# A gated hybrid block on one core: the first tile's convolution projection by seven products and at the end, the second tile's tokens scaled by way of DRAM, and pairs of units at the tile change

## The chip, the core and the metric

The kernel runs on one core of a Trainium2 chip. The metric is the device time of one execution in microseconds; the time of a kernel is the median of its runs. Engines are named as in the profile: PE is the matrix engine (TensorE), PEld its weight loads, DVE is VectorE, ACT is ScalarE, POOL is GpSimd and SP is SyncE, which here only issues DMAs. ACT and POOL issue DMAs too.

## The reference

One layer of a decoder block over 2048 positions and 1024 channels, in float32. Cut to what matters:

```python
h = rms_norm(x, norm_g)                                   # the scaled tokens
u = einsum('bsd,dc->bsc', h, w_in)                        # one input projection, split into:
v_c, b_c, c_c, z_c, q, k, v, z_a, gate_logits = split(u)
y_c = b_c * causal_depthwise_conv(c_c * v_c, conv_w)      # branch A: short gated convolution
y_c = y_c * silu(z_c)
y_a = y_c @ w_conv_out                                    # the convolution projection
q, k = rms_norm(q, q_norm_g), rms_norm(k, k_norm_g)       # branch B: attention over a window of 128
o = sliding_window_attention(q, k, v, sinks) * silu(z_a)
y_b = o @ w_attn_out                                      # the attention projection
g_a, g_b = split(sigmoid(gate_logits + gate_b))
return x + (g_a * y_a + g_b * y_b) @ w_out
```

## The kernel before, in words

**Precision.** Each operand is split into a high part (a cast on ACT) and a low part (a subtraction on DVE), and each block product is three matmuls: high by high, high by low, low by high. `op_split` and `form` make the operands ("op" tiles, 28 buffers), `two` inside `pieces_of` makes the weights' parts (8 buffers of 128x1024).

**Seven products.** A unit is a 1024 x 256 block of a weight matrix against the 1024 tokens of a tile. With both sides in halves it needs eight half products; the kernel forms sums of halves on DVE and does it in seven (Winograd's form of Strassen's scheme). One *product* is one of the seven: four blocks of 128 by three matmuls, 12 matmuls of 128x512. `sunit` runs one unit's seven products in turn; `spair` runs two units in turn about, in the order 1, 2, 5, 6, 3, 7, 4. The operand sides of the seven, numbered 1 to 7, come from four raw quarters and from `first_sum`, `second_sum`, `third` and `last_sum`.

**Tiles and stages.** The 2048 positions are two tiles of 1024 (T), each with halves of 512 (H). For each tile the units run in this order: k and v (tile 0 has a by-token form of its own), q (4), the convolution's c, v and b (12), the branch gates `ga` and `gb` (8), the convolution's gate `z` (4), the attention's gate `za` (4), the attention projection `yb` (4), the convolution projection `ya` (4). The attention's 32 blocks of a tile lie between the products from q to z. After both tiles comes the output projection `o` (8 units). `y_a` and `y_b`, multiplied by their gates, are added up in DRAM (`mt`): `yb` is stored by SP, `ya` is added by a DMA that accumulates, issued by POOL. The gated convolution result `y_c` goes through DRAM (`ocd`).

**The convolution projection of tile 0** is the one that is not done by seven: `ya_unit`, `branch` and `mm_t` (L1467) run eight half sums per unit from 16 plain operands (`opa`), 96 matmuls per unit. In tile 1, `ya` goes by `y_units`, `spair` and `sunit`; its sums of quarters are made ahead in `csum` and kept in DRAM (`csd`), and `conv_op` loads them by POOL's queue.

**Order.** The order on every engine is the program's order, written out by hand: `put(n, f)` places work at tick n, and `run` advances one tick for each product, so a tick is one product of PE with what is placed beside it. At each tick `run` also takes one *piece* of weight preparation (`piece`) from a list that runs ahead of the units: the raw weights (1 MB for a unit, two buffers) are loaded by SP, and the pieces make high and low parts. `paired` marks units whose pieces are interleaved for `spair`; `held` and `HOLD` keep the pieces behind a pair back for some ticks. Units 0 and 1 of `yb` have weights that were split earlier and kept in DRAM (`prepare`, placed by PREP_A and PREP_B in the stage `z`).

**The tile change.** `next_tile`, started with the first `ya` unit of tile 0, makes the operands of tile 1: it loads the tokens by ACT's queue twice, as rows for the squares (`x_load`, `x_square`, eight of 128x1024) and transposed (`raw_load`, 16 of 128x512), takes the inverse roots on DVE in four chains, spreads them over the partitions by transposes on PE (`x_roots`, L821), copies them to SBUF, scales the transposed tokens on DVE (`norm_l`, `norm_r`), and then forms the 28 operands, all beside the 32 ticks of `ya`. The buffers "u" (`upool`, two) are shared by the convolution, by the gates' loads and by other pairs of tiles.

## Time and profile before

| | |
|---|---|
| median of 3 runs | 1905.79 us (1904.58 to 1906.34) |
| the profiled execution | 1905.38 us |
| its span, first to last instruction | 1903.6 us |
| mean granted clock of TensorE | 0.999 |
| DMA traffic | 402.22 MB, mean 211 GB/s |

The profiled execution's span is cut into views. The page has busy time by engine, the chain of work that ended last, and the costliest groups of instructions with their mean time. A view of windows gives busy times, the granted clock and the DMA engines' busy share in stretches of the span, all in us from its start. A view of lines groups instructions: line, engine, operation, out<-in, shapes, count, then busy us and mean ns of one, then idle time just ahead of them and what ended it. Numbers in the name of a buffer are left out. Tile 0 ends and tile 1 begins at 891.35 us; the last product of tile 1's `ya` ends at 1747.48 us.

### The profile page before, as it was taken

How to read it: one execution, taken by the hardware profiler on the slowest of the kernel's cores; microseconds unless marked ns; L12 is line 12 of the kernel's file. 1: busy time of each engine (PE TensorE's matmuls, PEld its weight loads, DVE VectorE, ACT ScalarE, POOL GpSimd, SP SyncE). 2: the span in 40 equal slices, each digit the busy share in tenths (PEclk: the TensorE clock that was granted, in tenths of full speed). 3: DMA queues.
4: the chain of work that ended last, by engine and by line, in shares of the span. 5: the costliest groups of instructions: out<-in, count | busy, mean ns of one | idle time of the engine just before them, and what ended most of it. 6: DMA issues, size and time to landing. Idle time of an engine off the chain costs nothing.

```text
span 1903.6 us, 27441 instructions
## 1 busy us (share of the span) xinstructions
PE 1893.0 (99%) x8670; PEld 1574.6 (83%) x8670; DVE 1547.5 (81%) x2620; ACT 987.1 (52%) x1967; POOL 589.8 (31%) x846
## 2 busy tenths in 40 slices
PE   9999999999999999999999999999999999999999
PEld 7888888888887888888888888888888888888887
DVE  7988898888888767658799899888888777787754
ACT  7665455456666444434565455556666434444321
POOL 2073335335655000011362344444555000121000
PEclk9999999999999999999999999999999999999999
DMA  8286555558777857895584654567788987779653
GB/s 294 80 236 179 166 161 172 167 184 241 244 240 232 288 185 245 280 275 134 155 233 128 179 175 148 170 199 226 238 249 265 302 281 263 281 190 270 211 176 110
DMA packets 222497, 402.22 MB, mean 211 GB/s; under 512 B 30032, under 2 KB 104784, under 8 KB 212880
## 3 DMA queue, kind: packets, MB, share of 16 engines
q1 hardware_dynamic: 188224, 313.10, 50.5%
q0 software_dynamic: 30528, 78.94, 15.9%
q10 hardware_dynamic: 3600, 8.42, 1.3%
q8 instruction: 69, 1.13, 0.2%
q14 instruction: 76, 0.62, 0.1%
HBM read 271.09 MB, written 129.25 MB: 210 GB/s over the span
## 4 chain that ended last, share of the span: by engine, by line
PE 60%; DVE 4%; DMA 2%; issue 2%; POOL 1%; ACT 1%; SPq 0%; DVEq 0%; POOLq 0%; ACTq 0%
PE Y L639 22%; PE ya L1467 4%; PE Xyb L639 2%; PE Vyb L639 2%; PE Vo L639 2%; PE Xo L639 2%; PE Vza L639 2%; PE Xza L639 2%; PE Xcv L639 2%; PE Vcv L639 2%; PE Xgb L639 1%; PE Xq L639 1%; PE Vq L639 1%; PE Vz L639 1%; PE Vya L639 1%
## 5 line engine op out<-in xcount | busy, mean ns | idle before, releaser
L1291 POOL DMA_DIRECT2D x<-fd x256 | 139.5, 551 | 122.7 <-DMA fd<-f 58.8
L1264 ACT ACTIVATE p<-s,st,rq 128x128 f32<-128x128 f32 x256 | 113.0, 450 | 1.3 <-DMA gd<-th 1.3
L1312 POOL TENSOR_SCALAR_AFFINE_SELECT xh<-xh 64x512 fp32r<-64x512 f32 x64 | 59.5, 929 | 160.7 <-DVE xl L277 116.0
L1284 POOL DMA_DIRECT2D fd<-f x64 | 36.9, 576 | 215.9 <-DVE f L277 183.4
L1550 POOL DMA_DIRECT2D mt<-tha x16 | 13.8, 861 | 253.3 <-DVE tha L277 225.0
L639 PE MATMUL Xcv<-oph,wcv_ah 128*128 128x512 f32 x256 | 79.1, 390 | 0.0
L1312 POOL TENSOR_SCALAR_AFFINE_SELECT xl<-xl 64x512 fp32r<-64x512 f32 x64 | 66.0, 1032 | 4.4
L1312 POOL TENSOR_SCALAR_AFFINE_SELECT yp<-xl 64x512 fp32r<-64x512 f32 x64 | 58.3, 911 | 3.1
L1312 POOL TENSOR_SCALAR_AFFINE_SELECT yp<-yp 64x512 fp32r<-64x512 f32 x64 | 57.0, 891 | 4.2
L277 DVE TENSOR_TENSOR o<-po,o 64x256 f32<-64x256 f32 x128 | 53.4, 417 | 4.1 <-ACT o L1341 3.1
L277 DVE SCALAR_TENSOR_TENSOR y<-u,cols,y 128x512 f32<-128x512 f32 x64 | 53.2, 832 | 3.8 <-ACT y L1378 2.7
L639 PEld LDWEIGHTS Xcv<-oph,wcv_ah 128*128 128x128 f32 x256 | 47.6, 188 | 9.7
L277 DVE TENSOR_TENSOR p<-p,st 128x512 f32<-128x512 f32 x64 | 50.3, 786 | 3.4
L468 ACT CAST wcv_sh<-wcv_raw 128x1024 fp32r<-128x1024 f32 x16 | 16.8, 1050 | 68.7 <-DVE wcv_raw L277 68.7
L1264 ACT ACTIVATION_READ_ACCUMULATOR p<-s,st,rq 128x1 f32 x256 | 50.6, 198 | 0.0
L1341 ACT COPY o<-po 64x256 f32<-64x256 f32 x128 | 47.1, 368 | 6.7 <-DMA wpd_yb<-wph_yb 2.7
L639 PE MATMUL Xcv<-oph,wcv_al 128*128 128x512 f32 x128 | 49.8, 389 | 0.0
L1069 POOL DMA_DIRECT2D q2d<-q_h x64 | 44.2, 690 | 17.5 <-ACT q_h L1064 8.1
L1069 POOL DMA_DIRECT2D q2d<-q_l x64 | 44.1, 689 | 14.4 <-DMA q2d<-q_h 4.1
L2038 POOL DMA_DIRECT2D oc<-ocd x12 | 6.5, 543 | 135.3 <-DMA wyb_sh<-wpd_yb 118.9
L277 DVE TENSOR_TENSOR wcv_raw<-wcv_raw 128x512 f32<-128x512 f32 x64 | 47.3, 758 | 1.1
L277 DVE STREAM_TRANSPOSE f<-p 128x512 f32<-128x512 f32 x64 | 45.5, 711 | 2.7 <-PE Y L639 0.2
(713 smaller groups left out, 6505.3 us busy)
## 6 DMA issues: line engine op xcount, KB each, us to landing
gd<-th SPq DMA_DIRECT2D x64, 256.0 KB, 2.8
wcv_raw<-in_w_units SPq DMA_DIRECT2D x16, 1024.0 KB, 5.4
q<-q2d SPq DMA_DIRECT2D x64, 256.0 KB, 5.5
v<-vd SPq DMA_DIRECT2D x128, 128.0 KB, 3.5
fd<-f POOLq DMA_DIRECT2D x64, 256.0 KB, 4.0
x<-fd POOLq DMA_DIRECT2D x256, 64.0 KB, 3.2
th<-gd SPq DMA_DIRECT2D x48, 256.0 KB, 4.9
wga_raw<-in_w_units SPq DMA_DIRECT2D x8, 1024.0 KB, 5.6
```

The costliest lines, as they stand in the source:

```text
L277: r = f(*args, **kw)
L468: return (lambda: nc.scalar.copy(hi, src), lambda: vec.tensor_tensor(out=lo, in0=src, in1=hi.bitcast(F32), op=ALU.subtract))
L639: nc.tensor.matmul(ps, lhsT=w[:, j, :], rhs=b[:, m, :], start=start and j == 0 and i == 0, stop=j == KP - 1 and i == 2, skip_group_check=n ...
L1069: nc.gpsimd.dma_start(q2d[t][j][half, q * 2 * HB : (q + 1) * 2 * HB, i, e, :], src[HALVES[e]].bitcast(F32).rearrange("p (b x) -> p b x", x ...
L1264: nc.scalar.activation(out=p[:, i, :], in_=sg[:, i, HD : 3 * HD], func=AF.Exp, bias=st[:, 1, i : i + 1], scale=rv[:, i // 2, i % 2 : i % 2 ...
L1284: nc.gpsimd.dma_start(fd, f)
L1291: nc.gpsimd.dma_start(x[QUADS[k]], src[k])
L1312: nc.gpsimd.affine_select(out=d4, in_=s4, pattern=[[0, 2], [-32 * sg, 2], [0, G], [-sg, 32]], compare_op=ALU.is_gt if prev else ALU.is_ge, ...
L1341: nc.scalar.copy(ov, pov[oth, :, e])
L1467: nc.tensor.matmul(ps, lhsT=w[:, j, cs], rhs=o[:, m, :], start=n == 0 and i == 0, stop=n == KC - 1 and i == 2)
L1550: nc.gpsimd.dma_start(mt[t][k, :, hs(q)], m, accum_op=ALU.add)
L2038: nc.gpsimd.dma_start(got, ocd[t][2 * j + src[0], :, hs(src[1])])
```

## The change

1. **`ya` of tile 0** is no longer run in tile 0. Both tiles' `ya` run behind tile 1's `yb`, tile 0's first, each by seven products: `y_units(0, 0, ...)` and `y_units(1, 0, ...)`, each a pair and two single units. `ya_unit`, `branch`, `mm_t`, `split_op` and the weights' kind "T" go. `csum` and `conv_op` serve both tiles, with their places in CSUM_0, CSUM_1, CONV_0 and CONV_1.
2. **Tile 1's tokens.** The squares move into tile 0's convolution stage (`next_stats`: loads by SP into the "u" buffers, ticks 106 to 131 of tile 0). One chain of roots instead of four; the spread roots stay in PSUM. Between ticks -20 and +1 of the stage `yb` the transposed tokens are loaded by SP in eight pairs, scaled on DVE three ticks later, and stored to DRAM (`xnd`) one tick after that. `raw_load` then loads the scaled tokens from `xnd`, by ACT's queue as before, between ticks +8 and +20; the operands are formed at ticks +16 to +36. The first product of tile 1 is at tick +29.
3. **Pairs.** `yb` 2 and 3 of tile 0 run as a second pair, and k and v of tile 1 run as a pair, whose weights come in finer pieces (`fine`, `alone`); k's V bank is taken from the scores' banks.
4. **Places.** The sums of attention operands have their own places for each tile (CA0, CA1), and HOLD, THS_AT, Z_AHEAD, K_AT, WO_FORM_AT, PREP_A and PREP_B are changed; tile 1's v is turned one tick later, and k's copies use the "u" buffers.

The core of the diff:

```diff
-K_AT = (1, 1, 4)
+K_AT = (1, 0, 2)
+V_TURN = 2
...
-THS_AT = 10
-HOLD = 10
+THS_AT = (9, 8)
+YB_PAIRS = (2, 1)
+HOLD = (9, 11, 7, 11, 9, 8, 9)
+STAT_AT = (105, 112, 116, 119, 121, 122, 125, 128)
+NX_WAIT = 3
+NX_SCALED = (-20, -19, -15, -14, -10, -8, -4, -3)
+ROOTS_AT = (-39, -37, -17, -8)
+NX_LOAD0 = (10, 9, 8, 11, 12, 8, 13, 12)
+NX_LOAD1 = (15, 15, 15, 14, 18, 17, 17, 20)
...
-PREP_A = (15, 18, 18, 20, 23, 24, 29, 40, 36, 38)
-PREP_B = (20, 28, 23, 29, 31, 32, 34, 33, 39, 41)
+PREP_A = (12, 15, 15, 17, 19, 24, 22, 27, 29, 33)
+PREP_B = (19, 26, 25, 26, 28, 33, 36, 35, 40, 38)
...
+        if n in fine:
+            return w, [(1, 0, lambda: alone(1, 0)), (1, 0, both(lambda: alone(2, 2), sums_first)),
+                       (2, 0, first), (2, 0, second), (1, 2, single)]
...
-        nc.scalar.dma_start(h, xt2[c * P : (c + 1) * P, t * T + q * H : t * T + (q + 1) * H])
+        nc.scalar.dma_start(h, xnd[c, :, hs(q)])
...
-    def mm_t(ps, u, half, opt, q, last):
-        cs = slice(half * P, (half + 1) * P)
-        for n, k in enumerate(YA_CHUNKS):
-            j, p = divmod(k, 2)
-            force(u, p)
-            hi, lo = ready[u][p]
-            o = opt[k, q]
-            for i, (w, m) in enumerate(((hi, 0), (hi, 1), (lo, 0))):
-                nc.tensor.matmul(
-                    ps, lhsT=w[:, j, cs], rhs=o[:, m, :],
-                    start=n == 0 and i == 0, stop=n == KC - 1 and i == 2)
...
-        for j in range(NJ):
-            if t + 1 < NT:
-                plan.append(("T", (w_co, j * UC), ("ya", t, j)))
-            else:
-                if j == 0:
-                    paired.add(len(plan))
-                at_(("ya", t, j))
+        for i in range(NT if t + 1 == NT else 0):
+            paired.add(len(plan))
+            for j in range(NJ):
+                at_(("ya", i, j))
...
+    def next_stats(t, n0):
+        st = x_state(t)
+        st["ss"] = consts.tile([P, NB], F32, name=f"ss{t}")
+        def ld(b):
+            st["x", b] = upool.tile([P, 2 * H + 2], F32, tag="u", name=f"x{t}_{b}")
+            r0 = t * T + b * P
+            nc.sync.dma_start(st["x", b][:, 0:D], x2[r0 : r0 + P, :])
+        def square(b):
+            x_square(st["x", b][:, 0:D], st["ss"], b)
+        for b, n in enumerate(STAT_AT):
+            put(n0 + n, lambda b=b: ld(b))
+            put(n0 + n + 2, lambda b=b: square(b))
...
+        def scaled(q, c, n):
+            u = []
+            def ld():
+                u.append(upool.tile([P, 2 * H + 2], F32, tag="u", name=f"xn{t}_{q}_{c}"))
+                nc.sync.dma_start(
+                    u[0][:, 0 : 2 * H].rearrange("p (c x) -> p c x", c=2),
+                    xt2[c * P : (c + 2) * P, t * T + q * H : t * T + (q + 1) * H].rearrange("(c p) x -> p c x", p=P))
+            def norm():
+                for e in range(2):
+                    x_norm(u[0][:, hs(e)], c + e, st["rb"][q])
+            def keep():
+                nc.sync.dma_start(
+                    xnd[c : c + 2, :, hs(q)].rearrange("c p x -> p c x"),
+                    u[0][:, 0 : 2 * H].rearrange("p (c x) -> p c x", c=2))
+            put(n, ld)
+            put(n + NX_WAIT, norm)
+            put(n + NX_WAIT + 1, keep)
...
-            run(sunit(("k", t), ops, fin_k(t)))
-            run(sunit(("v", t), ops, fin_v(t)))
+            run(spair([("k", t), ("v", t)], ops, [fin_k(t), fin_v(t)], PAIR, True))
+        else:
+            next_stats(1, t0)
...
-        rest = y_units(t, 1, att["ops"])
-        if t + 1 < NT:
-            rest += [(*ya_unit(t, j, opa, (0, 1)), ((0, 0), (1, 1)), 5) for j in range(NJ)]
-        else:
-            rest += y_units(t, 0, conv["ops"])
+        rest = y_units(t, 1, att["ops"], YB_PAIRS[t])
+        if t + 1 == NT:
+            for i in range(NT):
+                n1 = n0 + 7 * (NJ * i + NJ - 1)
+                for n, (m, j) in zip((CONV_0, CONV_1)[i], ((m, j) for m in (1, 2, 5, 6, 3, 7, 4) for j in range(KP))):
+                    put(n1 + n - 3, lambda i=i, n=n1 + n, m=m, j=j: conv_op(i, n, m, j))
+                rest += y_units(i, 0, conv[i], 1)
+            wo_side(n0 + 7 * (NJ * (NT + 1) - 1), x_state(NT))
```

More of the change, by code (lines that the diff above doesn't have):

```diff
@@ new lines, in pieces_of, with single, sums, f @@
+        summed = []
+        if kind == "P":
+            return w, [(2, 2 * h, lambda h=h: pair(h, (h, 0), (h, 1), f"p{h}")) for h in range(2)]
+        def single():
+            hl = wpool.tile([P, 2, KP, P], F32R, tag="w", name=f"{name}_d")
+            w[4] = (hl[:, 0], hl[:, 1])
+            return two(hl[:, 0], hl[:, 1], raws[2 * n + 1][:, 1, 1])
+        def sums():
+            raw = raws[2 * n]
+            def f():
+                summed.append(vec.chain(
+                    *added(n), lambda: sub(raw[:, 0, 0], raw[:, 0, 1], raw[:, 0, 0])))
+                summed.append(vec.chain(
+                    lambda: sub(raw[:, 1, 1], raw[:, 1, 1], raw[:, 0, 0]),
+                    lambda: sub(raw[:, 1, 0], raw[:, 1, 0], raw[:, 0, 0])))
+            return (lambda: None, f)
@@ new lines, in more, with sums_first, f @@
+        def more():
+            raw = raws[2 * n]
+            if len(summed) < 2:
+                summed.append(vec.chain(
+                    lambda: sub(raw[:, 0, 1], raw[:, 1, 1], raw[:, 0, 0]),
+                    lambda: sub(raw[:, 1, 0], raw[:, 1, 0], raw[:, 0, 0])))
+        def sums_first():
+            raw = raws[2 * n]
+            def f():
+                summed.append(vec.chain(
+                    *added(n), lambda: sub(raw[:, 0, 0], raw[:, 0, 1], raw[:, 0, 0])))
+            return (lambda: None, f)
@@ new lines, in first, with second @@
+        def first():
+            summed[0]()
+            put(tick[0] + MORE_AT, more)
+            return (*pair(0, 6, 5, "s"), LO_BEHIND[0])
+        def second():
+            more()
+            summed[1]()
+            hi, lo = (v.rearrange("p (i j c) -> p i j c", i=2, c=P) for v in wpair(f"{name}_t"))
+            for i, m in enumerate((7, 3)):
+                w[m] = (hi[:, i], lo[:, i])
+            both = raw_of[n].rearrange("p k h x -> p (k h) x")[:, 1:3]
+            return (*two(hi.rearrange("p i j c -> p i (j c)"), lo.rearrange("p i j c -> p i (j c)"), both),
+                    LO_BEHIND[1])
@@ L644, in product @@
         d.add(n)
-        live[0] -= sum(c for m, c in USES if n in m and m <= d)
+        live[0] -= 1 if u in fine and n in (1, 2) else sum(c for m, c in USES if n in m and m <= d)
     def spare(name):
@@ L1980, in block_kernel @@
         zs[0][3]()
+        if t + 1 < NT:
+            next_tile(t + 1, tick[0] + 7 * 2 * NJ)
         if t + 1 == NT:
```

397 lines of the change are left out of this document (163 added, 234 removed).

## The prediction, made before the result was known

> **What bounds the kernel now.** I read the page first, its engine row and the shares of the chain of work that ended last.
>
> ```profile
> span 1903.6 us, 27441 instructions
> PE 1893.0 (99%) x8670; PEld 1574.6 (83%) x8670; DVE 1547.5 (81%) x2620; ACT 987.1 (52%) x1967; POOL 589.8 (31%) x846
> PE 60%; DVE 4%; DMA 2%; issue 2%; POOL 1%; ACT 1%; SPq 0%; DVEq 0%; POOLq 0%; ACTq 0%
> ```
>
> TensorE is busy 99% and the chain is nearly all TensorE. A busy PE proves little, so I then read the chain in order of time (start, us, what) for the pace.
>
> ```profile
> 802.64 10.88 PE ya L1467 x48
> ...
> 891.35 2.72 PE Xk L639 x12
> ...
> 1671.32 10.88 PE Xya L639 x48
> ...
> 1747.48 10.88 PE Xo L639 x48
> ```
>
> One product (12 matmuls) takes 2.72 us, 48 matmuls take 10.88: 0.2267 us each, unbroken. The convolution projection of tile 1, 28 products by seven per unit, runs from 1671.32 to 1747.48: 76.16 us, exactly 28 x 2.72. That of tile 0, eight half sums of 12 matmuls for each of four units, runs from 802.64 to 891.35: 88.71 us, where 32 x 2.72 is 87.04. So the bound is the number of matmuls, as long as VectorE, ScalarE and the DMAs stay ahead. How near they are to not doing so is in the table of windows (us of the window, then busy us of PE, PEld, DVE, ACT, POOL, the granted clock, DMA share, GB/s):
>
> ```profile
> 260.00:360.00 100.00, 100.00 (x478) 84.16 (x478) 89.26 (x157) 53.62 (x129) 38.65 (x55) 1.00 0.56 178
> ...
> 650.30:726.50 76.20, 76.20 (x338) 63.10 (x337) 53.78 (x78) 35.27 (x57) 0.00 (x0) 1.00 0.65 217
> 726.50:802.60 76.10, 76.10 (x337) 63.00 (x337) 57.34 (x85) 34.54 (x55) 0.00 (x0) 1.00 0.76 256
> 802.60:891.30 88.70, 88.53 (x394) 72.68 (x393) 63.65 (x134) 28.02 (x44) 12.92 (x15) 1.00 0.80 226
> 891.30:929.50 38.20, 38.20 (x174) 31.64 (x173) 31.00 (x59) 20.07 (x37) 3.40 (x5) 1.00 0.30 82
> ...
> 1100.00:1250.00 150.00, 149.21 (x700) 124.36 (x699) 135.78 (x223) 79.91 (x182) 66.05 (x90) 1.00 0.52 163
> ...
> 1671.00:1747.40 76.40, 76.40 (x339) 63.26 (x338) 58.50 (x84) 35.11 (x53) 15.72 (x21) 1.00 0.86 237
> ```
>
> VectorE at 89% (260 to 360) costs PE nothing; at 91% (1100 to 1250) it costs 0.79 us in 150. That is the tightness which the change has to live with.
>
> **The change part by part.** *Seven products for tile 0.* Four units of 96 matmuls become four of 84: 48 matmuls fewer, **10.88 us off PE**, by the chain's first row. The gaps in the old stage go too. It holds 88.71 - 87.04 = 1.67 us beyond its matmuls; part of that are two groups of four transposes of the roots, which stay:
>
> ```profile
> 830.00 0.60 PE L821 MATMUL ptr<-ident,rt 128*128 128x128 f32 x4
> 830.35 0.71 PE L1467 MATMUL ya<-opa,wya_0h 128*128 128x512 f32 x2
> ```
>
> The next matmul starts 0.35 us behind them, so 0.7 for both, and **0.97 us of gaps** is what can go (between 0 and 0.97; I take all of it, since the pace of 1671 to 1747 has none).
>
> *Its work at the end of tile 1.* 28 operand splits instead of 16, weights by sums, and 16 subtractions with 16 loads and 16 stores on SP for the sums of the gated convolution. The new stage is a copy of 1671 to 1747, in which the splits for the next stage, the weights' sums and the outputs together take VectorE 58.50 us of 76.40, and PE does not stop. The added subtractions:
>
> ```profile
> L277 DVE TENSOR_TENSOR cr<-cr,cr x16: 681/686/692, 1513.6 to 1567.6; 128x512 f32<-128x512 f32 x16
> ```
>
> 16 x 0.686 = 11.0 us for one tile; one tile's go where this tile's went, the other's are spread over the two stages behind, 5.5 us in each: 64 of 76. 28 operand loads and 16 accumulating stores go by POOL's queue, busy 15.7 of 76.4 us in that window. The sums that the output projection of tile 0 reads are now complete one stage, 76 us, ahead of it. Cost nothing, PE's 76 us hide it; without that cover at most the 11 us.
>
> *The tile change without its 88.7 us.* From 726.5 to 929.5 VectorE has 57.34 + 63.65 + 31.00 = 152.0 us of work in 203.0. What leaves this stretch, by groups of VectorE and ScalarE between 802.6 and 891.3:
>
> ```profile
> L277 DVE SCALAR_TENSOR_TENSOR h<-h,cols,rb 128x512 f32<-128x512 f32 x16 | 11.5, 747 | 0.0
> L277 DVE TENSOR_TENSOR opa<-ocr,opa 128x512 fp32r<-128x512 f32 x6 | 3.8, 685 | 0.0
> L277 DVE TENSOR_TENSOR wya_0l<-wya_raw,wya_0h 128x1024 fp32r<-128x1024 f32 x3 | 3.7, 1222 | 2.2 <-ACT wya_0h L468 2.2
> L302 DVE TENSOR_TENSOR hr_t<-hr_r 128x2 f32<-128x2 f32 x12 | 1.9, 161 | 0.4
> ...
> L811 ACT ACTIVATE xsq<-x 128x1024 f32<-128x1024 f32 x8 | 8.2, 1027 | 13.8 <-DMA tha<-gd 13.7
> ```
>
> 16 scalings by 0.747 = 12.0 (to the attention gate's stage, `za`); 16 operand splits by 0.685 = 11.0 and 16 outputs of about the same, 11.0; eight low parts of weights by 1.222 = 9.8; four root chains of 13 small operations by 0.161 = 8.4 (one chain, 2.1, comes back in `za`). Together 52. What stays is 100 us in 203.0 - 88.7 = 114.3: **87%**. In `za`, 53.78 + 12.0 + 2.1 = 67.9 of 76.2: **89%**. Neither is more than what 260 to 360 carries without a stop. By the rate of 1100 to 1250 (0.79 in 150) the two stages, 190 us, may lose 1.0 us; I take **1.0 us**, between 0 and what the rivals say.
>
> *Statistics in tile 0's convolution.* Eight squares of 1.03 us leave ScalarE's stretch at the change for ticks 106 to 131, where it is 54% busy; eight loads of 512 KB move from ACT's queue to SP's, at a DMA share of 0.56. Each square stands two ticks, 5.4 us, behind its load, and behind it on ScalarE are the copies out of PSUM that PE's third product waits for. Cost nothing; if a load takes the 6.1 us of the row below, 0.7 us eight times.
>
> *Tokens by way of DRAM.* Eight loads and eight stores of 512 KB are added on SP between ticks -20 and +1 of the output stage; the 16 loads of scaled tokens stay on ACT's queue. The scaling waits on VectorE three ticks (8.2 us) behind its load; queued behind it are the weights' low parts and the addition into PSUM which PE's later products need. The stores wait on SP for the scaling, and SP's weight loads stand behind them. What such loads take in a crowded stage (802 to 870: issues, KB each, us to landing):
>
> ```profile
> h<-in_xt ACTq DMA_DIRECT2D x16, 256.0 KB, 6.0
> x<-in_x ACTq DMA_DIRECT2D x6, 512.0 KB, 6.1
> wya_raw<-in_w_conv_out SPq DMA_DIRECT2D x2, 512.0 KB, 9.3
> wk_raw<-in_w_units SPq DMA_DIRECT2D x1, 1024.0 KB, 10.9
> ```
>
> Between 0 and 2.7 us of wait (10.9 - 8.2) for each, 1.1 by the 512 KB row of 9.3; I take 0, by the row of the same size that also reads tokens, 6.1.
>
> *Pairs.* `yb` 2 and 3, and k and v, run their products turn about: the same 28 and 14 products. Their weights must be ready two units at a time, but each product now has 2.72 us more until the next of its unit. Cost 0, the risk is the second rival.
>
> Sum: 1905.38 (the profiled execution: 1903.6 of span, 1.78 around it) - 10.88 - 0.97 + 1.0 = 1894.5. The median of the runs shown, 1905.79, is 0.41 above that execution: **1895.0 us**.
>
> **The rivals.** *A stop in the convolution gate's stage goes.* Before, PE stands at 612 us, for POOL's masks:
>
> ```profile
> 613.78 0.38 PE L1329 MATMUL po<-yp,v 128*128 128x256 f32 x1 [1.32 <-POOL yp L1312]
> 614.60 0.40 PE L1329 MATMUL po<-xl,v 128*128 128x256 f32 x1 [0.44 <-POOL xl L1312]
> ```
>
> ```profile
> 615.65 4.01 PE Y L639 x12
> ```
>
> ```profile
> 614.00:616.00 2.00, 1.56 (x7) 1.30 (x7) 1.05 (x2) 0.32 (x1) 0.55 (x1) 0.71 1.10 276
> 616.00:618.00 2.00, 2.00 (x6) 1.52 (x5) 0.00 (x0) 1.65 (x4) 0.00 (x0) 0.50 0.93 360
> 618.00:620.00 2.00, 2.00 (x10) 1.67 (x9) 0.23 (x1) 0.00 (x0) 0.00 (x0) 0.94 1.01 289
> ```
>
> 1.76 us of stop, and then a granted clock of 0.50, at which the next product takes 4.01 instead of 2.72: 3.1 us in all. The preparation of the output weights starts three ticks sooner, beside this place, so it may move either way; against its going: VectorE's order ahead of it is unchanged. Gone, it gives 1891.9. [...]
>
> *The change is too tight for two units of weights.* The raw weights of k and v come into the two buffers that `yb` 2 and 3 leave with their last piece, about tick 22; 10.9 us are four ticks, so tick 26 for k and up to 28 for v, while v's first piece is due on ScalarE at tick 26 and its product at 30. ScalarE, and VectorE behind it, would stand one to two ticks, 2.7 to 5.4 us, and PE 1 to 3 of it in two places: with the clock 4 to 8 us, 1899 to 1903, about 1901. For it: those 10.9 us; against it: 82 GB/s from 891 to 929, where loads have the engines to themselves.
>
> *Slower: the scaling loads land late.* Place: `za`. 16 x 256 KB read and written again are 8.4 MB in 60 us, 140 GB/s on top of 217: 357. The stage before runs at its DMA limit with less:
>
> ```profile
> 632.00:650.30 18.30, 18.30 (x82) 15.15 (x81) 14.68 (x22) 7.73 (x13) 0.00 (x0) 1.00 0.99 335
> ```
>
> If loads then land in 10.9 us, VectorE stands 8 x 2.7 = 21.6 us, `za` has 76.2 - 67.9 = 8.3 free, and 13.3 come onto PE, with half clock behind at least two stops 2.6 more: 1894 + 15.9 = 1910. It decides from a landing of 8.2 + 8.3 / 8 = 9.2 us. Against it: the 6.1 and 6.0 us rows come from a stage with a share near 1, too. [...]
>
> **How the numbers follow.** Forecast 0.60 (1893.5 to 1897.5); the stop at 612 gone 0.07 (1891.9); the tight change 0.18, of which 0.03 end above 1902; the late loads in part, 1902 to 1909.6, 0.05, in full, 1910, 0.10. What a measurement of this kernel can tell from no change is about 0.2%, 3.8 us: faster is below 1902.0, slower above 1909.6. Faster 0.60 + 0.07 + 0.15 = 0.82, same 0.08, slower 0.10. The range from 1890.5 to 1902.5 holds the first three cases but for 0.03; its lower end is the case without the stop at 612 and without the 1.0 us of allowance (1890.9).
>
> **What would show it.** Right: 8622 matmuls, no group of L1467, a projection of tile 0 that takes 76.2 us behind tile 1's `yb`, k's first product 76.2 us behind the first of `yb`, VectorE near 68 us in `za` and below 90% over the change. Wrong: chain rows of more than 2.75 us per product around the change or in `za`; a granted clock of 0.5 there; landings of the token loads over 9 us; VectorE's scaling with idle time ended by a DMA.

## The result, and the profile after

The changed kernel takes 1917.15 us (median of 4 runs, 1915.99 to 1917.68), the kernel before 1905.48 in the same session (1904.58 to 1906.34): ratio 1.006, 95% interval 1.0043 to 1.0078. It is 11.7 us slower, where about 10.5 us faster was forecast. The profiled execution took 1915.99 us.

From the head of the changed kernel's page (span, engines, DMA traffic, the chain's shares):

```profile
span 1914.3 us, 27564 instructions
...
PE 1884.9 (98%) x8622; PEld 1564.2 (82%) x8622; DVE 1578.9 (82%) x2643; ACT 1004.1 (52%) x1995; POOL 606.1 (32%) x874
...
DMA packets 230817, 422.14 MB, mean 221 GB/s; under 512 B 30928, under 2 KB 105680, under 8 KB 220688
...
PE 76%; DVE 7%; DMA 7%; issue 5%; ACT 3%; POOL 2%; SPq 1%; DVEq 0%; ACTq 0%; POOLq 0%
```

The 48 matmuls are gone (8622), and PE's busy time is 8.1 us less, not the whole 10.88. But PE idles 1914.3 - 1884.9 = 29.4 us, where it idled 1903.6 - 1893.0 = 10.6: 18.8 more, and 18.8 - 8.1 = 10.7 is the change of the span. The chain, 60% PE and 2% DMA before, says 76% and 7%; as it follows another way back through the program, its shares are a hint at most.

The same windows view as in the prediction finds the idle time. First three stretches around the forecast's own tests (`za`, tile 0's `yb`, the start of tile 1), then the eight that hold most of what PE lost (us of the window, then busy us of PE, PEld, DVE, ACT, POOL, granted clock, DMA share, GB/s):

```profile
652.80:729.00 76.20, 76.20 (x342) 63.09 (x341) 60.76 (x88) 32.69 (x52) 0.00 (x0) 1.00 0.81 268
729.00:813.00 84.00, 81.63 (x354) 65.78 (x353) 74.25 (x116) 36.02 (x61) 0.00 (x0) 1.00 0.79 270
813.00:880.00 67.00, 66.87 (x302) 54.82 (x301) 50.81 (x89) 35.63 (x62) 21.16 (x33) 1.00 0.43 122
...
360.00:395.00 35.00, 32.42 (x151) 26.68 (x150) 27.61 (x48) 22.82 (x50) 14.54 (x19) 1.00 0.65 198
590.00:640.00 50.00, 47.19 (x208) 38.11 (x208) 43.27 (x72) 29.98 (x56) 21.67 (x25) 0.97 0.81 268
725.00:745.00 20.00, 18.09 (x77) 13.76 (x76) 15.52 (x25) 8.03 (x15) 0.00 (x0) 1.00 0.93 325
780.00:840.00 60.00, 59.41 (x261) 48.03 (x261) 53.91 (x83) 31.45 (x53) 2.47 (x4) 1.00 0.43 145
875.00:910.00 35.00, 29.81 (x128) 23.34 (x127) 30.43 (x58) 19.01 (x33) 23.70 (x37) 1.00 0.95 273
1385.00:1400.00 15.00, 11.84 (x55) 9.75 (x54) 10.17 (x15) 7.39 (x14) 8.84 (x11) 1.00 0.80 252
1640.00:1712.00 72.00, 68.49 (x299) 55.43 (x298) 53.94 (x78) 32.31 (x50) 26.12 (x41) 1.00 0.96 288
1775.00:1785.00 10.00, 8.70 (x37) 6.65 (x36) 6.78 (x11) 4.51 (x8) 0.00 (x0) 1.00 1.13 345
sum 297.00, PE 275.95 PEld 221.74 DVE 241.63 ACT 155.51 POOL 97.35; mean PE 34.49 PEld 27.72 DVE 30.20 ACT 19.44 POOL 12.17
```

Width less PE's busy time is the loss: 21.05 us of the 29.4 in these eight. It is no single place, and `za`, where the forecast's slower rival stood, loses nothing. It does not follow VectorE's load either: busy 27.61 of 35 us, 15.52 of 20, 10.17 of 15, it is at 68% to 90% in these eight.

Who stands, and for what, is in the view of waits. ScalarE (ACT) from 360 to 395, 1380 to 1400 and 1650 to 1680, VectorE (DVE) from 860 to 912, and SP's queue from 700 to 745 and from 1640 to 1665 (us in total, times, longest):

```profile
ACT x L849 <- DMA x<-in_x: 7.6, 2, 3.8
...
ACT zs L1477 <- DMA ocd<-zin: 6.9, 1, 6.9
...
ACT wya_ah L495 <- DMA wya_raw<-in_w_units: 6.2, 1, 6.2
...
DVE k_t L308 <- DMA krb<-krd: 4.2, 2, 3.4
...
SPq L1911 <- DMA xnd<-xn: 7.9, 3, 5.6
...
SPq L1505 <- DMA mt<-th: 10.5, 2, 9.8
```

In each row an engine has come, in the order in which the program gives it its work, to a piece whose data have not landed (a transfer lands when its data are there): the statistics' squares, z's gate behind a store, the last pair's weights, k's spread roots, and on SP two kinds of loads that need a buffer whose store has not landed. PE stands a little later, for what is queued behind (in the first of these places 3.8 us behind the landing, at 384.7). The timeline of SP's queue shows the same for transfers. The start of `yb` (start, us, ...):

```profile
706.46 8.44 SPq L470 DMA_DIRECT2D wyb_raw<-in_w_units  x2
714.95 1.93 SPq L1920 DMA_DIRECT2D xnd<-xn  x2
722.52 2.52 SPq L1911 DMA_DIRECT2D xn<-in_xt  x2
725.13 0.42 SPq L516 DMA_DIRECT2D wyb_ah<-wpd_yb  x1
725.60 0.42 SPq L516 DMA_DIRECT2D wyb_al<-wpd_yb  x1
...
1647.81 3.85 SPq L1960 DMA_DIRECT2D csd<-cr  x3
1661.60 1.16 SPq L1505 DMA_DIRECT2D th<-gd  x2
1662.86 0.43 SPq L470 DMA_DIRECT2D wya_raw<-in_w_units  x1
```

The token loads `xn` wait for one of two buffers, that is for the store `xnd` of the pair of tokens that had it; the fetches of `yb`'s prepared weights, which need neither, stand behind them until 725.13. They land in 7.3 us (median of the two of `wyb_ah`), and the product that reads them is due at 731. There PE itself waits for them, from 722 to 745 (us in total, times, longest):

```profile
PE Xyb L674 <- DMA wyb_ah<-wpd_yb: 1.0, 1, 1.0
PE Xyb L674 <- DMA wyb_al<-wpd_yb: 0.9, 2, 0.5
```

That is all of the 1.91 us lost at this place. At 1661.60 two gate loads have waited 9.8 us for a buffer, and the last pair's raw weights go out behind them.

### The profile page after: what moved, and what is told of

It is laid out like the page before. It is cut to its first block, busy times and chain, and to the rows that moved or that the text cites. A ratio compares the mean times of both kernels' runs of the same rounds, so it can differ in the third digit from the quotient of the medians.

```text
span 1914.3 us, 27564 instructions
## 1 busy us (share of the span) xinstructions
PE 1884.9 (98%) x8622; PEld 1564.2 (82%) x8622; DVE 1578.9 (82%) x2643; ACT 1004.1 (52%) x1995; POOL 606.1 (32%) x874
## 3 DMA queue, kind: packets, MB, share of 16 engines
q8 instruction: 69, 1.13, 0.2%
## 4 chain that ended last, share of the span: by engine, by line
PE 76%; DVE 7%; DMA 7%; issue 5%; ACT 3%; POOL 2%; SPq 1%; DVEq 0%; ACTq 0%; POOLq 0%
PE Y L674 29%; PE Xcv L674 3%; PE Vcv L674 3%; PE Xza L674 2%; PE Vza L674 2%; PE Vyb L674 2%; PE Xgb L674 2%; PE Vgb L674 2%; PE Xyb L674 2%; PE po L1371 2%; PE Vga L674 2%; PE Xga L674 2%; PE Vo L674 2%; PE Vb L674 2%; PE Xb L674 2%
## 5 line engine op out<-in xcount | busy, mean ns | idle before, releaser
L1210 POOL DMA_DIRECT2D vd<-v x16 | 9.9, 622 | 220.1 <-DVE v L308 219.9
L1520 POOL DMA_DIRECT2D mt<-th x32 | 27.8, 868 | 121.7 <-DVE th L308 117.7
L1972 POOL DMA_DIRECT2D oc<-ocd x24 | 14.6, 654 | 146.1 <-ACT ophc L339 119.5
L674 PE MATMUL Y<-oph,wcv_d 128*128 128x512 f32 x192 | 46.9, 393 | 1.7 <-DVE vr L308 1.5
```

What stands on the lines that cost most here:

```text
L674: nc.tensor.matmul(ps, lhsT=w[:, j, :], rhs=b[:, m, :], start=start and j == 0 and i == 0, stop=j == KP - 1 and i == 2, skip_group_check=n ...
L1520: nc.gpsimd.dma_start(to, m, accum_op=ALU.add)
L1972: nc.gpsimd.dma_start(got, ocd[t][2 * j + src[0], :, hs(src[1])])
```

## The experiments

Theory one: the loads and stores that the change adds or moves land later than their fixed leads in ticks allow, or hold back others behind them on the same queue; the costs are the stops behind them. The rival: the shortened tile change and the pairs leave VectorE no room. Times are medians with the ratio's 95% interval to the kernel before on the same chip (1904.1 to 1905.3 us). "Idle" is span less PE's busy time, by each page's first rows; a loss at a place is the width of a window there less PE's busy time.

### One lead at a time

k's scaling two ticks later:

```diff
-K_AT = (1, 0, 2)
+K_AT = (1, 0, 4)
```

> The changed kernel with k scaled four ticks behind its spread loads instead of two. In the profile of the changed kernel VectorE stands 4.2 us for these loads (3.4 and 0.8) and PE loses 6.4 us between 882 and 913 (1.8, 3.3, 0.3, 0.8, 0.2 beyond its pace). Theory of late landings (fixed leads in ticks are shorter than what loads take to land, ScalarE or VectorE stands in order, and PE behind them): these 6.4 us go, 1917.2 becomes about 1911, and nothing else changes. Rival, VectorE has too much work in the shortened tile change: the wait is only where the lag shows, VectorE has no room, PE loses 4 to 6 us in the same stretch all the same: 1915 to 1917.

1916.98 us (1.005 to 1.008). VectorE's wait for `krb` falls from 4.2 us to 1.1, but most of the stop does not go: the windows below. The time is where the rival had it. The squares one tick further behind their loads:

```diff
-            put(n0 + n + 2, lambda b=b: square(b))
+            put(n0 + n + 3, lambda b=b: square(b))
```

> The changed kernel with the squares of the next tile's rows three ticks behind their loads instead of two. ScalarE stands 7.9 us for these loads in the profile of the changed kernel, 3.8 of it at 377 to 381, and PE loses 1.5 us each at 372 and 385, 2.3 us more than before there. Late landings: the ScalarE wait falls under 2 us and PE gets about 2 us back, 1915. Rival, ScalarE's added work (9.9 us) is what delays it there: the squares cost the same wherever they stand, no change, 1917.

1916.13 us (1.0049 to 1.0079). ScalarE's wait falls from 7.6 to 3.6 us and PE's loss from 360 to 395 from 2.58 to 1.13. The sums of tile 1's gated convolution left out, tile 0's read in their place:

```diff
-                for i in range(NT):
+                for i in range(1):
...
-                nc.gpsimd.dma_start(got, csd[t][(5, 7, 6, 4).index(m), j])
+                nc.gpsimd.dma_start(got, csd[0][(5, 7, 6, 4).index(m), j])
```

> The changed kernel without the sums of tile 1's convolution results: their 16 loads, 16 subtractions and 16 stores are left out, and tile 0's sums are loaded in their place, so that part of the result is another. In the changed kernel the DMA engines are 99% busy from 1595 to 1673, weights of 1 MB land in 9.4 us, and PE loses 4.5 us between 1648 and 1708 and 1.8 at 1781. Late landings: 8.4 MB less in that stretch brings the weights' landing to about 6 us, VectorE and ScalarE stand no longer for DMAs there, and about 4 of the 4.5 us come back: 1913. Rival, VectorE's 11 us of subtractions are the cost: PE gets the time back too, but ScalarE's 6.2 us wait for the weights at 1667 to 1673 stays in the trace. Rival two, what is late are the weights alone, because their buffers come free late: nothing changes, 1917.

1917.09 us (1.0047 to 1.0078). ScalarE's wait for `wya_raw` stays at 6.2 us: SP comes to that load only 2.0 us sooner (62.2 us behind the first product of tile 0's `ya`, 64.1 in the change), again behind four gate loads (1644.04 to 1665.24 us). PE's loss from 1640 to 1712 falls from 3.51 to 2.06. The second load of z one tick sooner, as it was before:

```diff
-Z_AHEAD = (7, 5)
+Z_AHEAD = (7, 4)
```

> The changed kernel with the loads of tile 1's second and third convolution gate units at the fourth tick again, as before, instead of the fifth. In the changed kernel ScalarE stands 6.9 us at 1383 to 1390 for a buffer whose store to DRAM has not landed; that store stands on SP behind four such loads, and PE loses 3.4 us. Late landings by queue order: with the loads a tick sooner the store goes out sooner, ScalarE's wait falls to the 3.4 us of before, PE gets 3 us back, 1914. Rival, the store is late because its gate is computed late: the wait stays, 1917.

1916.49 us (1.005 to 1.0084). ScalarE's wait for the store falls from 6.9 to 2.8 us, PE's loss there from 3.16 to 1.30 (1380 to 1400). Three of the four moved their wait the expected way, the sums did not, and none moved the time by more than its interval of 3 us either side. Idle fell from 29.4 to 27.5, 25.7, 27.9 and 26.4, while PE's busy time rose from 1884.9 to between 1885.1 and 1889.3: what a stop gives back was partly taken by a lower granted clock, in the mean 0.999, 0.997, 0.996 and 0.997 in these four profiles and 0.999 in the change's (last section).

### Queue or room

k multiplied by itself, so that VectorE does as many operations of the same size with no load to wait for (the roots' spread and the true scaling are left out):

```diff
-                put(tick[0] + K_AT[1] + 2 * n, lambda i=i, q=q: spread(i, q))
...
-            mul(kt, kt, rbs[i, q])
+            mul(kt, kt, kt)
```

> Tile 1's and tile 0's k are multiplied by themselves instead of by the spread roots, and the 8 loads of spread roots (krb) are left out; VectorE does the same number of operations of the same size. The change lost 6.4 us of PE between 880 and 910 us. Theory one (the work behind the pair k and v stands for landings): VectorE no longer waits there for krb, PE's loss between 880 and 910 falls from 6.4 to below 2 us, time about 1912. Rival (VectorE has no room there, since k's and v's ends now fall together beside the first q): the multiplications still stand in front of q's weights, VectorE is busy over 90% of those windows, PE still loses 4 us or more, time 1915 to 1918.

1915.35 us (1.0042 to 1.007), which is the rival's range; theory one said 1912. The place says otherwise. The q stage, 870 to 910 us, in the changed kernel, with k's scaling later, and with no spread loads:

```profile
870.00:910.00 40.00, 34.81 (x150) 27.49 (x149) 32.75 (x61) 22.03 (x38) 28.58 (x44) 1.00 0.92 264
```

```profile
870.00:910.00 40.00, 36.20 (x150) 28.82 (x149) 34.66 (x65) 21.43 (x37) 29.31 (x45) 0.96 0.95 276
```

```profile
870.00:910.00 40.00, 38.78 (x168) 30.85 (x167) 36.89 (x68) 24.69 (x42) 31.08 (x49) 1.00 0.91 256
```

PE loses 5.19, 3.80 and 1.22 us, and VectorE is busy 32.75, 34.66 and 36.89: busiest, 92%, where least is lost. The same stage of the kernel before, with k and v one behind the other, lost nothing with VectorE busier still:

```profile
949.00:989.00 40.00, 40.00 (x178) 33.05 (x177) 37.44 (x69) 25.91 (x45) 27.86 (x43) 1.00 0.88 239
```

The rival falls as the main cause at this place: VectorE has room for the work, but not while it stands. Something of it stays: with k's work put later (second row) the loads are waited for 1.1 us only, and PE still lost 3.80, at the end of a chain that is mostly VectorE's own work (15.1 of the 19.2 us from 884.8 to 904.1).

The token loads and stores on POOL's queue:

```diff
-                nc.sync.dma_start(
+                nc.gpsimd.dma_start(
                     u[0][:, 0 : 2 * H].rearrange("p (c x) -> p c x", c=2),
...
-                nc.sync.dma_start(
+                nc.gpsimd.dma_start(
                     xnd[c : c + 2, :, hs(q)].rearrange("c p x -> p c x"),
```

> The eight loads of tokens and the eight stores of scaled tokens are issued on POOL's queue instead of SP's; the bytes are the same. Theory one (prepared weights of yb stand on SP behind the token stores, which wait for VectorE): the fetches of yb's first weights go out near 711 us again instead of 725, the stops at 731 to 737 us (2.7 us of PE) go, time about 1914. Rival (the stretch has too many bytes: the queue makes no difference): the fetches land as late as before, the stops stay at 2 us or more, time 1916 to 1918.

1920.4 us (1.007 to 1.0099), no faster than the change, and above both forecasts. The first fetch goes out at 716.56 instead of 725.13, as theory one has it, yet PE's loss from 725 to 745 fell only from 1.91 to 1.38, and VectorE stands 2.9 us for `xn`. In the twelfth run (below), with the tokens on the same queue, PE waits at this place for operands of ScalarE and VectorE instead of the fetches (1.0 us each), and the loads of `xn` wait on POOL 14.4 us for the stores that free their buffers. Operand and output weight loads two ticks sooner:

```diff
-                    put(n1 + n - 3, lambda i=i, n=n1 + n, m=m, j=j: conv_op(i, n, m, j))
+                    put(n1 + n - (3 if i and m in (5, 7, 6, 4) else 5), lambda i=i, n=n1 + n, m=m, j=j: conv_op(i, n, m, j))
...
-WO_AHEAD = 3
+WO_AHEAD = 5
```

> The operand loads of the convolution projections go out two ticks (5.4 us) sooner, except those of tile 1's sums, and the loads of the output projection's weights two ticks sooner. Theory one (leads in ticks shorter than the landings): the stops at 1649, 1676 and 1707 us (4.3 us of PE) and the 1.85 us at 1781 fall to 2 us together, time about 1913. Rival (the landings themselves grow, since the same bytes go through a stretch at a DMA share of 0.99: what is asked for sooner only displaces another load): the stop at 1676, which ends with raw weights, stays at 2 us or grows, the sum stays above 4 us, time 1916 to 1918.

1919.28 us (1.0061 to 1.0099), above both forecasts. At their places both were right: the output projection's loss from 1775 to 1785 went to nothing (10.00 of 10.00 busy), and the one from 1640 to 1712 grew from 3.51 to 6.27, where the DMA engines are busy 0.96. That what is asked for sooner displaced other loads there is the rival's reading; which loads, was not followed up.

All of these at once, with the first, second and fourth run's edits (no diff of its own):

> All at once: k's scaling two ticks later, squares three ticks behind their loads, the second load of z one tick sooner, token loads and stores on POOL's queue, operand loads and output weights two ticks sooner. Theory one (many short stops, each from one load or queue, with half clock behind some of them): the gains add, PE loses 8 to 12 us less than in the change, time 1904 to 1909. If the stops only move (VectorE and the DMAs have no room over long stretches), time 1913 to 1918, with PE's losses at other places but the same sum.

1919.66 us (1.0062 to 1.0089): no gain, and above both forecasts. PE loses 3.39 us from 1635 to 1650 (0.59 in the change), where the sooner operand loads are. Without those, the rest the same:

> The change with k's scaling two ticks later, squares three ticks behind their loads, the second load of z one tick sooner, token loads and stores on POOL's queue and output weights two ticks sooner: the eighth run without its sooner operand loads, which had brought a stop of 3.6 us at 1642. Theory one (short stops that each have a cause of their own): PE's stops 8 us fewer than in the change, time 1906 to 1911. If stops only move: 1914 to 1918.

1913.08 us (1.0027 to 1.0052), idle 21.8: 4 us better than the change, still slower than before, and between the two forecasts.

### Leaving out what was added

No spread loads (as in the fifth run), no trip of the tokens through DRAM (as in the tenth, below), no sums of tile 1 (as in the third), z's load as in the fourth, and no statistics loads or squares; every product stays, in the changed order and pairs:

```diff
+        nc.vector.memset(st["ss"], 1024.0)
...
-            put(n0 + n, lambda b=b: ld(b))
-            put(n0 + n + 2, lambda b=b: square(b))
```

> Left out: the eight statistics loads and squares (a constant stands for the sums), the trip of the tokens through DRAM with its 16 scalings (the operands come from the unscaled tokens), tile 1's four sums of the gated convolution (tile 0's are read instead), the spread loads of k's roots; the second load of z goes one tick sooner, as before the change. All 8622 products of PE stay, in the changed order and pairs. Theory one (the loss is in the loads and stores that the change adds or moves and in what stands behind them): PE's stops fall by 10 us or more and the time comes to 1896 to 1904, below the kernel before. Rival (the shorter tile change and the pairs cost the time by themselves, VectorE and weights): 1910 or more.

1903.73 us (11 runs; 0.9985 to 1.0003), idle 19.5: 13.4 us less than the change, level with the kernel before. With the transfers, this run also leaves out the work on their data (16 scalings, 16 subtractions, eight squares), so by itself it does not part the two. The trip alone left out of the change:

```diff
-        for i, n in enumerate(NX_SCALED):
-            scaled(i // KP, i % KP * 2, n0 + n)
...
-        nc.scalar.dma_start(h, xnd[c, :, hs(q)])
+        nc.scalar.dma_start(h, xt2[c * P : (c + 1) * P, t * T + q * H : t * T + (q + 1) * H])
```

> Left out: the eight loads, eight stores and 16 scalings of the tokens' trip through DRAM; tile 1's operands come from the unscaled tokens by the same 16 loads on ACT's queue. Theory one: SP has no token loads or stores in front of yb's weight fetches, the stops at 731 to 737 us (2.7 us of PE) and those of z at 631 us (0.9) go, those in the attention and q stages stay, time about 1913. Rival (the trip costs nothing, the fetches are late by yb's second pair of weights): the stops at 731 to 737 stay above 2 us.

1915.9 us (1.0039 to 1.0076). The stop at the start of `yb` is gone (20.00 of 20.00 busy from 725 to 745), that of z from 620 to 640 stays (0.64 against 0.61), so the trip is not its cause. The whole time, less by 1.2 us, does not show the gain. And the kernel before, with `Z_AHEAD = (7, 5)` for `(7, 4)`:

> The kernel before with one number of the change alone: the second load of z in tile 1 one tick later (5 for 4). Theory one (a lead one tick shorter meets a landing that is longer): PE stops near 1388 us by 2 to 3.5 us, with 1.7 us more where half clock follows, time 1907 to 1909. Rival (the stop of the change there comes from its own additional traffic): no stop above 0.8 us, time 1904 to 1906.

1905.86 us (0.9999 to 1.0017). From 1455 to 1475, the kernel before and this one:

```profile
1455.00:1475.00 20.00, 19.45 (x93) 16.01 (x92) 16.65 (x23) 11.81 (x20) 10.67 (x13) 1.00 0.81 261
```

```profile
1455.00:1475.00 20.00, 17.77 (x85) 14.71 (x84) 15.08 (x22) 10.10 (x18) 10.33 (x12) 1.00 0.81 265
```

One tick costs 1.68 us of PE at the place; the 1.2 of the time are within the noise. The change's 3.16 is more. Next, the raw weights of the convolution projections on POOL's queue, first in the change, then, with output weights sooner, on the ninth run's kernel:

```diff
-                nc.sync.dma_start(both.rearrange("p k h x -> p (k h x)"), w_units[unit_index(key)])
+                (nc.gpsimd if key[0] == "ya" else nc.sync).dma_start(
+                    both.rearrange("p k h x -> p (k h x)"), w_units[unit_index(key)])
```

> One edit: the raw weights of the convolution projections are loaded on POOL's queue instead of SP's, where the load for the last pair stood behind two gate loads that wait for a buffer until a store has landed (issued 1662.86, 11.4 us ahead of the pair). Theory one (an in-order queue passes one wait on to the next load): the load goes out some 5 to 10 us sooner, ScalarE's wait for wya_raw (6.2 us) goes below 2, the stop at 1676 us (2.96) falls below 1. Rival (it lands late since the DMA engines are full, share 0.99): ScalarE still waits over 4 us, the stop stays over 2 us. The time alone can tell little: 1913 to 1917.

1920.45 us (1.0079 to 1.0116). PE's loss from 1670 to 1690 went from 2.69 to nothing, the one from 1590 to 1650 grew from 0.59 to 4.52: these loads now stand in POOL's queue, which waits for VectorE in its turn (from 1560 to 1670, 23.7 us for `th`, 10.8 and 8.6 us for parts of weights). The last pair's load did not go out sooner, as theory one had it (65.2 us behind the first product of tile 0's `ya`, 64.1 in the change); it landed in 7.8 us instead of 10.0, and ScalarE's wait halved to 3.2. So SP's order is seen in the timeline of the change, but this run does not show it to be the cause of the stop, and POOL's order is no better.

> The ninth run (statistics loads, the tokens' trip, tile 1's sums and k's spread loads left out, second load of z as before), with the output weights two ticks sooner and the raw weights of the convolution projections on POOL's queue. Theory one: the stops that were left there at 1661 to 1694 (3.9 us) and at 1754 to 1770 (3.0) go too, and the time comes to 1896 to 1899, to within 2 to 4 us of the forecast 1895, which counts only products. Rival (the shorter program has a bound of its own behind the loads, so other stops grow): 1901 or more.

1898.21 us (median of 8, 1895.89 to 1900.8; ratio 0.996 to 0.998), 0.3% faster than the kernel before. Its profiled execution took 1896.11, where the forecast's sum of products says 1894.5. Its span and engines, the windows of the losses, and SP's queue ahead of `yb`:

```profile
span 1894.4 us, 27363 instructions
...
PE 1880.2 (99%) x8622; PEld 1563.9 (83%) x8622; DVE 1562.2 (82%) x2612; ACT 996.1 (53%) x1979; POOL 610.8 (32%) x882
```

```profile
360.00:395.00 35.00, 34.51 (x163) 28.88 (x162) 30.28 (x51) 20.79 (x47) 16.32 (x22) 1.00 0.53 156
...
720.00:800.00 80.00, 79.48 (x349) 65.14 (x348) 70.54 (x109) 37.57 (x63) 0.00 (x0) 1.00 0.73 248
...
870.00:910.00 40.00, 38.76 (x168) 30.86 (x167) 37.80 (x77) 24.80 (x43) 29.69 (x46) 1.00 0.92 253
1570.00:1710.00 140.00, 139.86 (x617) 115.52 (x616) 108.65 (x154) 65.06 (x98) 48.19 (x75) 1.00 0.91 258
```

```profile
709.65 0.42 SPq L517 DMA_DIRECT2D wyb_ah<-wpd_yb  x1
```

The pairs, the change without its 88.7 us, and both convolution projections run with little loss (0.52 us in 80, 1.24 in 40, 0.14 in 140), VectorE at 88% and 95% in the first two (70.54 of 80, 37.80 of 40). The fetches go out at 709.65, not 725. The change itself with such shifts (the twelfth run's edits, with `K_AT = (1, 0, 3)`, the token trip one tick sooner, and the raw weights on POOL's queue):

> A version that computes the whole: k's scaling one tick later, squares three ticks behind their loads, second load of z one tick sooner, token loads and stores on POOL's queue and one tick sooner, output weights two ticks sooner, raw weights of the convolution projections on POOL's queue. Theory one: the twelfth run (1913.1) less the stop at 1676 (3.0) and part of those at 737 to 739 (2.6) and 903 (3.8, half clock within): 1905 to 1910, near the kernel before. If stops only move: 1911 to 1916.

1918.89 us (1.0058 to 1.0085), idle 28.5: the stops moved, as the rival had it, and the time is above even its range (from 725 to 745 alone 3.72 us, at a mean clock of 0.83). Last, the additions put back on the fourteenth run's kernel:

> The fourteenth run (1898.2, profiled span 1894.4) with the trip of the tokens through DRAM put back: eight loads, eight stores, 16 scalings; the rest is still left out. Theory one (each addition costs where it stands, by its own stops): PE stops come back at 731 to 737 us (2.7) and nowhere else, time 1900 to 1903. Rival (the trip alone fits, the stops come only with the other loads): below 1899.5, no stop over 0.6 us at the start of yb.

1901.52 us (11 runs; 0.9978 to 0.9996): 3.3 more.

```profile
725.00:745.00 20.00, 18.21 (x77) 13.82 (x76) 15.57 (x25) 8.40 (x16) 0.00 (x0) 1.00 0.96 340
```

The 1.79 us at the start of `yb` are back, where the change has 1.91.

> The fourteenth run with tile 1's four sums of the gated convolution put back: 16 loads, 16 subtractions, 16 stores of 256 KB on SP and VectorE. Theory one: stops come back between the two convolution projections (1600 to 1710 us, 1 to 5 us of PE), since these loads and stores share SP and the DMA engines with gate loads and operands at a share of 0.99; time 1899 to 1904. Rival: below 1899.5.

1906.26 us (11 runs; 0.9994 to 1.0012): 8.1 more in the median, and three of the runs between 1900.8 and 1901.9, so between 3 and 9. VectorE's wait, and the window:

```profile
DVE cr L308 <- DMA cr<-ocd: 14.6, 5, 5.1
```

```profile
1575.00:1710.00 135.00, 126.75 (x550) 102.20 (x549) 111.16 (x163) 58.20 (x89) 46.66 (x73) 1.00 0.96 299
```

VectorE stands for the sums' operands, PE loses 8.25 us. Here the raw weights are on POOL's queue, where they wait for VectorE (10.9 and 8.1 us from 1570 to 1650); in the change itself, with SP's queue, leaving the sums out won little (third run). The 8 us are the sums with that queue, not the sums alone.

> The fourteenth run with the eight statistics loads and squares and the spread loads of k's roots put back. Theory one: stops come back at 372 and 385 us (2.3 us of PE) and in the q stage behind the pair (880 to 905, 4.3 us), time 1903 to 1906; with the other two runs and the second load of z (3.4 us) the parts then add up to the 19 us between the fourteenth run and the change. Rival: below 1901.

1904.1 us (11 runs; 0.9991 to 1.0008): 5.9 more. Windows of both places:

```profile
365.00:390.00 25.00, 23.16 (x109) 19.06 (x108) 19.42 (x33) 14.98 (x27) 10.42 (x13) 1.00 0.74 218
870.00:910.00 40.00, 34.56 (x147) 27.01 (x146) 35.98 (x67) 22.77 (x39) 25.61 (x40) 1.00 0.90 264
```

1.84 and 5.44 us, near the change's 2.58 (from 360 to 395) and 5.19. Put back one by one, the additions cost 3.3 + 8.1 + 5.9 = 17.3 us of the 18.9 between the medians of the fourteenth run and the change (by the ratios 0.17%, 0.33% and 0.30%, 15 us of 17). That the sum comes so near is in part chance: the 8.1 was measured with the raw weights on POOL's queue, which the change does not have, and the load of z and the two shifts of loads, in which the fourteenth run also differs from the change, are not in the sum.

## Why the prediction was wrong

The sum took the matmuls and gaps off, 11.85 us, and put 1.0 us on for all that the change adds or moves. The matmuls came off; in place of the 1.0, PE idles 18.8 us more. The step that failed is that every added or moved transfer was priced at nothing where the engine that works on its data had room: four times "cost nothing", "I take 0" or "cost 0". What the runs showed in its place are stops for single transfers that land late, or go out late behind others on their queue. Part by part:

*Products.* Right: 8622 matmuls, and where the additions are left out and some loads shifted (fourteenth run), the time comes to within 1.6 us of the sum (1896.11 against 1894.5 for the profiled execution), in the median within 3.2 (1898.21 against 1895.0).

*"Statistics ... Cost nothing; if a load takes the 6.1 us of the row below, 0.7 us eight times."* Failed. The eight loads land in 4.2 us in the median, less than the 5.4 of their lead, but in 3.2 to 8.2: two of them, with 8.2 and 6.7, held ScalarE 3.8 us each, and PE lost 2.58 from 360 to 395, where it lost 0.46 before. The cover, ScalarE at 54%, was no cover: in the chain of work, 1.22 us of the loss go back from PE over VectorE and ScalarE's cast of weights (`wb_d`) to the square that stood in front of it.

*"Tokens ... Between 0 and 2.7 us of wait ... I take 0."* VectorE stood 2.0 us in all for `xn`, and `za` lost nothing. But the same paragraph says that "SP's weight loads stand behind them", and it priced that at nothing. This is where the step failed most plainly: it cost 1.9 us of PE at the start of `yb`, and 1.8 there and 3.3 of time when put back. What was late was not the token but the transfer queued behind it.

*"Its work at the end of tile 1 ... Cost nothing."* Failed, by the 3.51 us from 1640 to 1712 and 1.30 at the output projection. VectorE was estimated at 64 of 76 and has room (53.94 of 72). The raw weights of the last pair stood on SP behind two gate loads, landed in 10.0 us at a DMA share of 0.96, and held ScalarE 6.2 us. The added sums are only part of it: without them (third run) that wait was as long, and 2.06 of the 3.51 us stayed. What the rest would take is open. At the output projection it was the lead: with the weights two ticks sooner (seventh run) its loss was gone.

*Pairs, "Cost 0".* From 813 to 880, where k and v run as a pair, the change lost 0.13 us, so the second rival's mechanism, two units' weights, did not come. What came with the pair is that k's roots are due two ticks behind their loads, three before, which land in 6.1 us in the median and up to 9.1, in a stage at 0.92: 5.2 us, the largest loss of one place. Without the loads 1.2 are left (fifth run); two ticks more of lead won back only 1.4 (first run). The diff's `K_AT = (1, 0, 2)` stood for it, and the prediction did not price it.

*Z_AHEAD 4 to 5* was not priced at all: 3.16 us at 1393.

*The allowance of 1.0 us* came from VectorE's busy share (89% loses nothing). The share did not tell which run loses: in the q stage, VectorE at 92% to 95% went with a loss of 1.2 us in 40, and at 82% with waits, of 5.2.

*The slower rival* had the right kind, loads that land late in front of an engine's next work, and the wrong place and decider: it needed landings of 9.2 us in `za`, and the token loads took 5.4 in the median and 8.7 at most; VectorE was busy 60.76 us there, not 67.9. The half clock in its price and in the second rival's (2.6 us behind two stops) rests on one stop of before, 4.01 against 2.72 us; the runs showed stops with it and without it (last section). Leads of 5.4 us elsewhere failed. *The first rival* did not come: the stop for POOL's masks stands, at 614 to 616.

What stays open: single fixes won back 1 to 3 us at their place and under 2 in the time, others made it slower, while the additions cost more when put back; and the whole versions found no more than 4 us. Except for k's roots (fifth run) and the start of `yb`, where PE's wait names the fetches, no run parts the added transfers from the work on their data. Whether another order of these transfers would let all of them fit was not found. The pairs undone, one unit after the other, were not tried.

## What to carry to other kernels

When a step is moved or added off the critical path, price its loads and stores first: for each, the lead in time against the landing in that stage's own rows, and for each that waits (for a buffer, a result), what is queued behind it on the same queue. A busy share of the engine that does the work says little on this; in the q stage here the engine was busiest in the runs that lost least (92% to 95% with 0 to 1.2 us lost in 40, 82% to 91% with 3.8 to 5.4). A lead that just fits its landing became a stop here when the stage carried more bytes: of `yb`'s weights, fetched from 725.13 for a product due at 731.3, the first four fetches landed in 5.6 and 5.1 us before (medians of two each), and in 7.3 and 8.1 with the token trip beside them; from 725 to 745 the DMA engines' share was 0.93 with the trip and 0.60 without it (tenth run).

## What the runs showed of the hardware

Half clock followed one stop here, and did not follow a longer one. In the changed kernel, the stop at 614 to 616 us (1.31 and 0.44 us) and the longest stop, at 1390 to 1393 (3.16 us in one piece):

```profile
613.40:616.80 3.40, 1.65 (x8) 1.05 (x7) 3.32 (x5) 0.67 (x2) 2.92 (x3) 1.00 1.01 350
616.80:620.21 3.41, 3.41 (x11) 2.79 (x10) 1.47 (x3) 3.35 (x6) 0.00 (x0) 0.50 1.06 353
1389.90:1393.10 3.20, 0.04 (x2) 0.03 (x1) 1.29 (x2) 2.80 (x6) 1.59 (x3) 1.00 0.76 280
1393.10:1397.10 4.00, 4.00 (x18) 3.29 (x19) 3.92 (x8) 3.46 (x6) 0.10 (x1) 1.00 0.61 188
```

Behind the shorter the granted clock was 0.50 for 3.41 us, from 616.80 to 620.21; behind the longer it stayed at 1.00. In the kernel before, the stop at the same place (1.32 and 0.44 us) was followed by 0.50 as well. What decides whether half clock follows was not shown; the length of the stop alone does not tell it in these rows. Four stretches of half clock in the third run's profile (e3_no_csum1), each of 3.41 us again:

```profile
375.23:378.64 3.41, 3.41 (x10) 2.71 (x9) 1.15 (x2) 3.37 (x7) 0.00 (x0) 0.50 0.86 285
620.99:624.40 3.41, 3.41 (x9) 2.63 (x8) 0.42 (x1) 2.58 (x6) 0.00 (x0) 0.50 1.07 413
897.47:900.88 3.41, 3.41 (x9) 2.64 (x8) 3.34 (x7) 1.89 (x4) 2.27 (x4) 0.50 0.92 240
1679.12:1682.53 3.41, 3.41 (x9) 2.66 (x9) 3.41 (x7) 1.45 (x3) 2.50 (x4) 0.50 0.40 47
```

3.41 us at 0.50 are 1.7 us of full clock, so each of them costs about 1.7 us: an estimate from these rows. The times of one kernel spread over up to 9.7 us (1915.64 to 1925.30 in the seventh run, with mean clocks of 0.995 to 0.997). So a fix of 2 us is read here from the window of its place, not from the time.
